# An output projection in seven block products, weight sums made by DMA, and x tiles with rows of one length

## The chip, the cores and the metric

The kernel runs on one core of one Trainium2 chip. The metric is the device time of one launch in microseconds (us). The engines are TensorE (PE in the profile; its weight loads are PEld), VectorE (DVE), ScalarE (ACT), GpSimd (POOL) and SyncE (SP), which here only issues DMAs. Each engine works through its own list of instructions in a fixed order and waits in that order.

## What is computed

One layer: 512 tokens of width 2048 and 16 meta tokens ahead of them, 8 pairs of attention heads in a sliding window, 8 groups of a state-space mixer (SSD), an output projection and a norm. Cut to what matters here:

```python
h = concatenate([meta, x])                       # 528 rows, 2048 wide
proj = rmsnorm(h, norm_pre_w) @ w_in             # z, xbc, dt, q, k, v, gate
y   = ssd(silu(conv(xbc)), dt) ; y = rmsnorm_per_group(y * silu(z)) * ssd_norm_w   # 2048 wide
att = banded_sink_attention(rope(q), rope(k), v) * silu(g_att)                      # 1024 wide
mix = concatenate([y, att])                      # 512 tokens x 3072
out = x + rmsnorm(mix @ w_out, norm_post_w)      # w_out is 3072 x 2048
```

All of it is float32. A float32 product is made of three matmuls in a rounded format (fp32r): each operand is split into a rounded part (hi) and the rest (lo), and hi·hi, hi·lo and lo·hi are summed in PSUM.

## The kernel before

**Weights.** `w_in` is read as 68 tiles, each in two chunks of 512 KB, and `w_out` as 48 chunks. A chunk n is loaded by SP's queue into `st` (two buffers), ACT rounds it to `hi` (line 132), and DVE makes `lo` = st − hi (line 133); `hi` and `lo` have three buffers each. `use(n)` asks for the split of chunk n+2 and the load of chunk n+4 and hands chunk n to the matmuls.

**Stages.** A prologue normalises and transposes x into the resident tiles `xh` and `xl` (four tiles each, four of the 16 k-blocks to a tile; a tile's row is `X_ROW[q]` floats long, of which 528 are used). Then come the keys and values, 8 attention heads (pairs of heads, in fact; "head" below is one such pair), 8 SSD groups of two units, and the output projection. A head needs two `w_in` tiles, q and gate; each is one `project(False)` of 48 matmuls 512 columns wide (16 k-blocks, three terms, line 157), written to a PSUM bank `pa`. A tile for the SSD convolutions is `project(True)`: pairs of matmuls `pa` and `pb`, 272 and 256 columns wide.

**Side work of a head** (`attend`): when its q tile is complete, four ACT copies make `swq` (467), DVE applies rope (`qr`, 469 to 471), ACT and DVE split the result into `qs` (521, 522); PE makes the scores `sc` (541, 542); DVE takes maxima `mx`, ACT exponentials into `pbuf` (550), DVE divides (`pbuf`, 557); PE transposes (`ptm` 563, `ptp` 572), ACT copies them to `pt` (575); PE multiplies with v (`av`, 590), and DVE applies the gate (`ma`, 596).

**Side work of an SSD unit**: DVE and ACT make the decay tiles `R`; PE transposes x (`xp`), DVE scales it (`xd`, and `xe` on POOL), PE makes `yd` and the states' sums `stp`, DVE runs the recurrence over four blocks (`sta`), PE makes `yo`, and DVE gathers `yy`; each group ends with a mean square by PE (`ms`), a reciprocal and two products.

**Order.** The program's order interleaves side work with projections by a clock of its own: `tick(us)` advances it by each matmul group's planned time, `spawn` starts a task, and a task's `yield us` says when it goes on. The order on each engine is then made by the tile framework's scheduler when the kernel is built: it goes by its own estimate of when each instruction's inputs are there, those of DMAs too. On the chip the order is fixed.

**Output projection.** Four column blocks of 512 (r), each over 24 k-blocks and four token blocks (t) into four PSUM banks: 4 x 24 x 4 x 3 = 1152 matmuls 128x512 (line 880). The split activations `mh` and `ml` are made once, in the first block. After each block ACT squares and DVE multiplies by the norm's weights (894, 895); the last block ends token block by token block with `finish`.

The lines that the texts below speak of most:

```python
    def use(n):
        split_w(n + (2 if n == NCI else 3))
        load(n + 3 + NST)
        return ready.pop(n)
```

Of the kernel before, what the change touches and what calls it, by code (L numbers as in the profile page):

```python
# [15 lines left out]
P = 128  # L16
D = 2048
# [10 lines left out]
NST = 2  # L28

X_ROW = (640, 576, 544, 528)  # L30
# [13 lines left out]
def hybrid_layer(ctx, tc, x, pre, npre, w_in, w_dt, par, w_out, npost, cst, out):  # L44
# [25 lines left out]
    cw = cpool.tile([P, 32, 4], F32, name="cw")  # L70
# [39 lines left out]
    NCH = NCI + 4 * (NKO // 2)  # L110
    staged, ready = {}, {}
    nload, nsplit = [0], [0]

    def load(upto):
        while nload[0] < min(upto, NCH):
            n = nload[0]
            st = wpool.tile([P, 1024], F32, tag="st", bufs=NST, name=f"st{n}")
            if n < NCI:
                src = w_in[n // 2, :, 1024 * (n % 2):1024 * (n % 2 + 1)]
            else:  # L120
                src = w_out[(n - NCI) // (NKO // 2), (n - NCI) % (NKO // 2)]
            nc.sync.dma_start(st, src)
            staged[n] = st
            nload[0] += 1
# [12 lines left out]
    def use(n):  # L137
        split_w(n + (2 if n == NCI else 3))
        load(n + 3 + NST)
# [5 lines left out]
    for q in range(4):  # L145
        for xs_, nm in ((xhg, "xh"), (xlg, "xl")):
            xs_.append(xpool.tile([P, 4, X_ROW[q]], F32R, name=f"{nm}{q}")[:, :, 0:T])
# [35 lines left out]
    with sb("pro", side="right") as pp:  # L183
# [116 lines left out]
        with tc.manual_schedule(engines={ET.PE, ET.Activation, ET.DVE, ET.Pool}):  # L300
# [59 lines left out]
            nc.vector.tensor_scalar(cw.rearrange("p a b -> p (a b)"), pr[:, P_CW:P_CW + P], 0.5, None, ALU.mult)  # L360
# [25 lines left out]
    def steps():  # L386
# [42 lines left out]
        en = sp.tile([P, P], F32, name="en")  # L429
# [5 lines left out]
        ec = sp.tile([P, P], F32, name="ec")  # L435
# [65 lines left out]

    keys(0, pieces0)
# [9 lines left out]
    def attend(hp, pieces):  # L512
# [120 lines left out]
    pools = {}  # L633
# [54 lines left out]
    def unit_task(u_, xs, cT):  # L688
# [127 lines left out]
    mh, ml = [None] * NKO, [None] * NKO  # L816
    vpool.release()
    xpool.release()
    o1 = ctx.enter_context(sb("o1", reuse_waits="tile"))
    o2 = []  # L820
    xr = [None] * NT

    def o_pool(k):
        if k < 16:
            return o1
        if not o2:
            assert not tasks
            pools["s"].release()
            o2.append(tc.alloc_tile_pool(name="o2", bufs=1, side="right", reuse_waits="tile"))
        return o2[0]  # L830

    with tc.high_priority(offset=400):
        splitting([0, 1])
    npw = ssq = None
    ot = {}
    n3 = None
    NC = NKO // 2

    def finish(t, jk):

        b = 3
        rs = o1.tile([P, 2], F32, tag="ors", bufs=4, name=f"ors{t}")
        nc.vector.tensor_reduce(rs[:, 0:1], ssq[:, t, 0:3], AX.X, ALU.add)
        nc.vector.tensor_scalar(rs[:, 0:1], rs[:, 0:1], 1.0 / D, EPS, ALU.mult, ALU.add)
        nc.scalar.activation(jk, pss[t], AF.Square, accum_out=ssq[:, t, 3:4])
        nc.scalar.activation(rs[:, 1:2], ssq[:, t, 3:4], AF.Sqrt, bias=rs[:, 0:1], scale=1.0 / D)
        nc.vector.tensor_tensor(ot[b, t], pss[t], npw[:, b * 512:(b + 1) * 512], ALU.mult)
        nc.vector.reciprocal(rs[:, 1:2], rs[:, 1:2])
        for b in range(4):
# [127 lines left out]
```

## Time and profile before

| | us |
|---|---|
| median of 3 runs (lowest, highest) | 1206.51 (1205.87, 1207.91) |
| the profiled execution | 1206.65 |
| its span in the trace | 1204.9 |
| PE busy in the span | 1192.1 |
| DVE, ACT, POOL busy | 676.4, 442.8, 48.5 |
| output projection, first to last matmul | 935.4 to 1197.3 |

The span is what the trace covers; the profiled execution's time has 1.75 us more, outside of the trace. Times inside the trace count from the span's start. The attention stage lies at about 58 to 310 us and the SSD stage at about 310 to 935 us.

### The profile page before, as it was taken

How to read it: one execution, taken by the hardware profiler on the slowest of the kernel's cores; microseconds unless marked ns; L12 is line 12 of the kernel's file. 1: busy time of each engine (PE TensorE's matmuls, PEld its weight loads, DVE VectorE, ACT ScalarE, POOL GpSimd, SP SyncE). 2: the span in 40 equal slices, each digit the busy share in tenths (PEclk: the TensorE clock that was granted, in tenths of full speed). 3: DMA queues.
4: the chain of work that ended last, by engine and by line, in shares of the span. 5: the costliest groups of instructions: out<-in, count | busy, mean ns of one | idle time of the engine just before them, and what ended most of it. 6: DMA issues, size and time to landing. Idle time of an engine off the chain costs nothing.

```text
span 1204.9 us, 18243 instructions
## 1 busy us (share of the span) xinstructions
PE 1192.1 (99%) x7565; PEld 1058.1 (88%) x7565; DVE 676.4 (56%) x1196; ACT 442.8 (37%) x754; POOL 48.5 (4%) x84
## 2 busy tenths in 40 slices
PE   8999999999999999999999999999999999999997
PEld 6998888888999989999999899998998788888886
DVE  7655555555556766656658557576675922222325
ACT  7544544445422423424234233242332712121212
POOL 0000000000100001010000000100100000000000
PEclk9999999999999999999999999999999999999999
DMA  6332222222323233233333232323332423233534
GB/s 228 100 97 88 71 86 73 71 76 91 115 95 111 91 106 99 96 108 104 105 98 97 95 116 88 114 86 105 109 97 70 157 88 104 92 101 94 169 101 179
DMA packets 37045, 125.53 MB, mean 104 GB/s; under 512 B 4706, under 2 KB 5346, under 8 KB 36706
## 3 DMA queue, kind: packets, MB, share of 16 engines
q1 hardware_dynamic: 32864, 111.78, 28.5%
q0 software_dynamic: 4096, 12.59, 3.3%
q8 instruction: 59, 0.97, 0.3%
q14 instruction: 24, 0.19, 0.1%
q10 hardware_dynamic: 2, 0.01, 0.0%
HBM read 120.03 MB, written 4.33 MB: 103 GB/s over the span
## 4 chain that ended last, share of the span: by engine, by line
PE 98%; DMA 1%; DVE 0%; ACT 0%; SPq 0%; issue 0%; DVEq 0%
PE pa L157 48%; PE po L880 22%; PE pb L157 17%; PE yd L722 1%; PE av L590 1%; PE stp L732 1%; PE yo L745 1%; PE ptp L572 1%; PE xt L228 1%; PE sc L542 1%; PE cbp L649 1%; DMA x<-in_x 1%; PE xp L702 1%; PE sc L541 1%; PE stp L730 1%; PE warm L278 0%
## 5 line engine op out<-in xcount | busy, mean ns | idle before, releaser
L133 DVE TENSOR_TENSOR lo<-st,hi 128x1024 fp32r<-128x1024 f32 x182 | 222.7, 1224 | 379.9 <-ACT hi L132 376.7
L157 PE MATMUL pa<-xh,hi 128*128 128x272 f32 (+2 forms) x1088 | 374.7, 344 | 0.0
L157 PE MATMUL pa<-xl,hi 128*128 128x272 f32 (+2 forms) x1088 | 366.1, 336 | 0.0
L157 PE MATMUL pa<-xh,lo 128*128 128x272 f32 (+2 forms) x1088 | 365.8, 336 | 0.0
L132 ACT CAST hi<-st 128x1024 fp32r<-128x1024 f32 x182 | 191.4, 1052 | 471.6 <-PE po L880 169.0
L157 PEld LDWEIGHTS pa<-xh,hi 128*128 128x128 f32 x1088 | 205.5, 189 | 24.5 <-issue 3.9
L157 PEld LDWEIGHTS pa<-xh,lo 128*128 128x128 f32 x1088 | 205.4, 189 | 21.4
L157 PEld LDWEIGHTS pa<-xl,hi 128*128 128x128 f32 x1088 | 205.3, 189 | 19.0
L157 PE MATMUL pb<-xh,lo 128*128 128x256 f32 x576 | 162.6, 282 | 0.0
L157 PE MATMUL pb<-xl,hi 128*128 128x256 f32 x576 | 162.4, 282 | 0.0
L157 PE MATMUL pb<-xh,hi 128*128 128x256 f32 x576 | 162.3, 282 | 0.0
L880 PE MATMUL po<-hi,mh 128*128 128x512 f32 x384 | 149.5, 389 | 1.2 <-ACT mh L783 1.2
L880 PE MATMUL po<-lo,mh 128*128 128x512 f32 x384 | 149.4, 389 | 0.0
L880 PE MATMUL po<-hi,ml 128*128 128x512 f32 x384 | 148.9, 389 | 0.0
L157 PEld LDWEIGHTS pb<-xh,hi 128*128 128x128 f32 x576 | 108.5, 188 | 1.1
L157 PEld LDWEIGHTS pb<-xl,hi 128*128 128x128 f32 x576 | 108.4, 188 | 0.0
L157 PEld LDWEIGHTS pb<-xh,lo 128*128 128x128 f32 x576 | 108.4, 188 | 0.0
L880 PEld LDWEIGHTS po<-hi,mh 128*128 128x128 f32 x384 | 72.1, 188 | 16.2 <-ACT mh L783 1.4
L880 PEld LDWEIGHTS po<-lo,mh 128*128 128x128 f32 x384 | 72.1, 188 | 15.0
L880 PEld LDWEIGHTS po<-hi,ml 128*128 128x128 f32 x384 | 72.1, 188 | 15.0
L626 DVE SCALAR_TENSOR_TENSOR cv<-ub,cw,cv 128x528 f32<-128x528 f32 (+1 forms) x96 | 73.4, 764 | 2.4
L627 ACT ACTIVATE ct<-cv 128x528 f32<-128x528 f32 (+1 forms) x32 | 20.5, 641 | 67.1 <-DVE cv L626 67.0
(210 smaller groups left out, 1067.6 us busy)
## 6 DMA issues: line engine op xcount, KB each, us to landing
st<-in_w_in SPq DMA_DIRECT2D x136, 512.0 KB, 3.7
st<-in_w_out SPq DMA_DIRECT2D x48, 512.0 KB, 3.5
R<-scr POOLq DMA_DIRECT2D x32, 256.0 KB, 3.6
x<-in_x SPq DMA_DIRECT2D x8, 512.0 KB, 9.4
ev<-scr POOLq DMA_DIRECT2D x32, 128.0 KB, 3.0
out<-o SPq DMA_DIRECT2D x16, 256.0 KB, 2.4
xr<-in_x SPq DMA_DIRECT2D x8, 256.0 KB, 6.6
npw<-in_npost SPq DMA_DIRECT2D x1, 1024.0 KB, 4.4
```

The source lines that it names most:

```text
L132: nc.scalar.copy(hi, st)
L133: nc.vector.tensor_tensor(lo, st, hi.bitcast(F32), ALU.subtract)
L157: nc.tensor.matmul(ps, wt, xt[k][:, a:b], start=(k == 0 and j == 0), stop=(k == NKT - 1 and j == 2))
L228: nc.tensor.transpose(tp[:, kk, :], xts[j][:, k * P:(k + 1) * P], ident)
L541: nc.tensor.matmul(sv[:, c, o0:o1], lq, kh[:, kv, t0:t0 + o1 - o0], start=True, stop=False)
L542: nc.tensor.matmul(sv[:, c, o0:o1], lq, kl[:, kv, t0:t0 + o1 - o0], start=False, stop=True)
L572: nc.tensor.transpose(tp[:, sl * P:(sl + 1) * P], src, ident)
L590: nc.tensor.matmul(av[h * 64:h * 64 + 64, j * P:(j + 1) * P], lt, rh, start=(s_ == 0), stop=(s_ == 1))
L626: nc.vector.scalar_tensor_tensor(d, uu[:, tap + c0:tap + T], cw[:, ct, tap:tap + 1], d, ALU.mult, ALU.add)
L627: nc.scalar.activation(th[:, 0:n], d, AF.Tanh)
L649: nc.tensor.matmul(cbp[:, j * P:(j + 1) * P], bT[:, cs], cT[:, cs], start=True, stop=True)
L880: nc.tensor.matmul(pss[t], a[k][:, cs], w_, start=(k == 0 and i == 0), stop=(k == NKO - 1 and i == 2))
```

## The change

**Seven products.** mix and w_out are each seen as 2 x 2 blocks (tokens by k, k by columns), and the output's four blocks come from seven block products and sums (the Strassen-Winograd form) in place of eight products. A product p has 12 chunks, 2 token blocks, 2 k-blocks to a chunk and 3 terms: 7 x 144 = 1008 matmuls 128x512, 12 for a chunk in place of 24. So 84 chunks of 512 KB are loaded and split in this stage in place of 48, with four `st` buffers there in place of two. Activation blocks and their sums are split for each product (`held`), and `done` adds the products into the output's blocks, in PSUM and SBUF, ahead of the norm.

**Weight sums.** Four of the seven products need sums of blocks of w_out. They are made in DRAM (`wsum`) during the attention stage: 24 copies of 1 MB by SP's queue and 24 accumulating DMAs of 1 MB by POOL's queue, in three tasks of six moves, 30.0 apart on the program's clock. The copies are kept in program order on SP.

**x tiles.** All eight have rows of 576 floats (2304 bytes), in place of 640, 576, 544 and 528 (2560, 2304, 2176 and 2112 bytes). Some constants share space.

```diff
-X_ROW = (640, 576, 544, 528)
+X_ROW = 576
...
-    NCH = NCI + 4 * (NKO // 2)
+    NCH = NCI + 7 * KH
...
+    W_SRC = [w_block(0, 0), wsum[1], w_block(1, 0), wsum[0], wsum[2], w_block(1, 1), wsum[3]]
...
-            st = wpool.tile([P, 1024], F32, tag="st", bufs=NST, name=f"st{n}")
+            if n % 4 > 1 and "o" in pools:
+                st = pools["o"].tile([P, 1024], F32, tag="st", bufs=2, name=f"st{n}")
+            else:
+                st = wpool.tile([P, 1024], F32, tag="st", bufs=NST, name=f"st{n}")
...
+    def weight_sums(c):
...
+        w11, w12, w21, w22 = [w_block(r, q) for r in range(2) for q in range(2)]
+        for moves in (((2, w22, None), (0, w12, None)), ((2, w12, ALU.add), (0, w11, ALU.add)),
+                      ((1, wsum[2], None),), ((1, w11, ALU.add),), ((3, wsum[1], None),), ((3, w21, ALU.add),)):
+            for d, src, op in moves:
+                for b in range(2):
+                    to, fr = wsum[d, b, c:c + 2], src[b, c:c + 2]
+                    if op is None:
+                        tc.keep_in_program_order(nc.sync.dma_start(to, fr))
+                    else:
+                        nc.gpsimd.dma_start(to, fr, accum_op=op, max_dma_last_dim=4096)
+            yield 30.0
+
+    for c in range(0, KH // 2, 2):
+        spawn(weight_sums(c), 6.0 + 25.0 * c)
...
+    def held(p, i):
...
+        if p == 1:
+            sums(i)
+        elif p == 4:
+            nc.vector.tensor_tensor(h1[:, :, HI], h1[:, :, LO], h1[:, :, HI], ALU.subtract)
+        elif p == 5:
+            nc.vector.tensor_tensor(s2[i], s2[i], h2[:, :, LO], ALU.subtract)
+        src = (h1[:, :, LO], s2[i], h2[:, :, LO], s1[i], h1[:, :, HI], s2[i], h2[:, :, HI])[p]
...
+        nc.scalar.copy(ah, src)
+        nc.vector.tensor_tensor(al, src, ah.bitcast(F32), ALU.subtract)
...
+    def done(p, t, b, ps):
...
+        elif p == 4:
+            c = oo[t + 2, b + 2] = o_tile(f"c22_{t}_{b}")
+            nc.vector.tensor_tensor(c, vv[t, b], ps, ALU.subtract)
+            nc.vector.tensor_tensor(uu[t, b], ps, uu[t, b], ALU.subtract)
+            weigh(t + 2, b + 2, c)
...
+        else:
+            if b == 1:
+                presum(t + 2)
+            c = oo[t + 2, b] = uu[t, b]
+            nc.vector.tensor_tensor(c, ps, c, ALU.add)
+            weigh(t + 2, b, c)
+            if b == 1:
+                finish(t + 2, 1)
```

**What stands where on the engines.** The scheduler's order in the attention stage and the first SSD groups is another one, since it reckons with the new DMAs. First PE, at the third head's scores (`sc_0_1656`; in the kernel before these scores are `sc_0_1637`). Before, from the end of its q tile (`pa_1456`):

```order
L157 MATMUL pa_1456<-xh_98,hi_1367 128x512
L157 MATMUL pa_1456<-xl_99,hi_1367 128x512
L157 MATMUL pa_1456<-xh_98,lo_1368 128x512
L157 MATMUL pa_1562<-xh_92,hi_1457 128x512
L157 MATMUL pa_1562<-xl_93,hi_1457 128x512
L157 MATMUL pa_1562<-xh_92,lo_1458 128x512
```

The gate's tile `pa_1562` follows here, 39 of its 48 matmuls with `av` of the head before among them, then the scores, the gate's last 9 and 33 of the next tile, and only then the transposes. After the change PE has this, in the first piece from the end of the q tile (`pa_1470`), in the second from the end of the scores:

```order
L171 MATMUL pa_1470<-xh_98,hi_1381 128x512
L171 MATMUL pa_1470<-xl_99,hi_1381 128x512
L171 MATMUL pa_1470<-xh_98,lo_1382 128x512
L573 MATMUL sc_0_1656<-kh,qs_1575 128x80
L574 MATMUL sc_0_1656<-kl,qs_1575 128x80
```

```order
L573 MATMUL sc_3_1686<-kh,qs_1575 128x192
L574 MATMUL sc_3_1686<-kl,qs_1575 128x192
L595 MATMUL ptm_1770<-ident,pbuf 16x128
L604 MATMUL ptp_0_1775<-ident,pbuf 128x128
L595 MATMUL ptm_1770<-ident,pbuf 16x128
```

The scores stand right behind the q tile that they are made from, the transposes right behind the scores, and `av` right behind the transposes, with the whole gate tile (`pa_1580`) after them. Counted for all eight heads: the projection matmuls between q and scores, scores and first transposes, last transposes and `av` were 48, 42, 21 for the first head, 36 to 39, 42, 21 for the second to the seventh, and 39, 75, 12 for the eighth. They are now 48, 42, 21 for the first; 36, 12, 0 for the second; 0, 0, 0 for the third and the fifth; 39, 9, 0 for the fourth; 39, 42, 6 for the sixth; 0 (`av` of the sixth alone is between), 0, 0 for the seventh; and 39, 75, 12 for the eighth.

Second ACT, at the copies of the second head's transposes (`pt`). Before, and then after:

```order
L132 CAST hi_1457<-st_1310 128x1024
L605 ACTIVATE gt_1453<-pa_1305 128x512
L132 CAST hi_1487<-st_1371 128x1024
L575 COPY pt_0_1509<-ptp_0_1504 128x512
L575 COPY pt_1_1516<-ptp_1_1511 128x512
L575 COPY pt_2_1532<-ptp_2_1527 128x512
L575 COPY pt_3_1537<-ptp_3_1534 128x256
```

```order
L638 ACTIVATE gt_1467<-pa_1319 128x512
L607 COPY pt_0_1527<-ptp_0_1522 128x512
L607 COPY pt_1_1534<-ptp_1_1529 128x512
L607 COPY pt_2_1550<-ptp_2_1545 128x512
L607 COPY pt_3_1555<-ptp_3_1552 128x256
L146 CAST hi_1320<-st_1228 128x1024
L146 CAST hi_1381<-st_1258 128x1024
```

The next chunks' casts have moved behind the copies; the subtractions that make `lo` stand behind them on DVE, for the second and the fourth head behind the gate product `ma` too, which reads `av`. The casts stand so at the second to the fifth and at the seventh head.

Third DVE, in the first SSD group. Before, the recurrence `sta` of the first unit is followed by a convolution and chunks' subtractions; after the change, 18 subtractions and 17 operations of convolutions stand ahead of it, 720 projection matmuls stand on PE between the first and the second row of `stp`, and behind it comes:

```order
L147 TENSOR_TENSOR lo_4682<-st_4525,hi_4681 128x1024
L769 COPY sta_3582<-stp_3577 128x128
L772 SCALAR_TENSOR_TENSOR sta_3582<-sta_3582,cdec,stp_3577 128x64 x6
L716 TENSOR_SCALAR R_0_3664<-R_0_3664,acs 128x128 x2
L742 TENSOR_TENSOR xd_3768<-xp_3759,dt 128x512
L781 TENSOR_TENSOR ev_3503<-yo_3692,ev_3503 128x512
L739 TENSOR_TENSOR xmd_3766<-xm_3764,dtm 16x128
L782 TENSOR_TENSOR yy_3557<-yy_3557,ev_3503 128x512
L758 SCALAR_TENSOR_TENSOR yy_3814<-cv_3656,pr,yd_3805 128x512
```

Four units' chains stand one behind the other there, with 123 DVE operations (4 of them subtractions for chunks) against 217 projection matmuls on PE, up to the first transpose of the fifth unit (`xp_5062`). From the third group on the order is as before.

## Rows read from the trace of the kernel before

**Rows 1.** The page, part 1: busy time of each engine.

```profile
PE 1192.1 (99%) x7565; PEld 1058.1 (88%) x7565; DVE 676.4 (56%) x1196; ACT 442.8 (37%) x754; POOL 48.5 (4%) x84
```

**Rows 2.** Waits of PE in the whole span: total, times, longest.

```profile
PE nw L295 <- DMA nwr<-in_npre: 2.7, 1, 2.7
PE xt L228 <- DVE x L219: 1.3, 1, 1.3
PE po L880 <- ACT mh L783: 1.2, 1, 1.2
```

**Rows 3.** The chain that ended last, 158 to 216: start, us, what.

```profile
159.24 0.04 PE sc L541
...
161.00 9.65 PE pa L157 x42
170.65 0.22 PE ptm L563 x2
170.87 0.87 PE ptp L572 x8
...
173.84 0.66 PE ptp L572 x6
...
179.31 2.04 PE av L590 x32
```

**Rows 4.** Timeline of DVE, 148 to 184: start, us, engine, line, operation.

```profile
164.40 1.84 DVE L557 TENSOR_SCALAR pbuf<-pbuf,sm 128x80 f32<-128x80 f32 x8
...
181.40 0.69 DVE L596 SCALAR_TENSOR_TENSOR ma<-av,gs 128x512 f32<-128x512 f32 x1 [0.19 <-PE av L590]
182.13 1.41 DVE L522 TENSOR_TENSOR qs<-qr,qs 64x512 fp32r<-64x512 f32 x2
```

**Rows 5.** Timeline of ACT, 148 to 184.

```profile
171.35 1.08 ACT L575 COPY pt<-ptp 128x512 f32<-128x512 f32 x2 [1.85 <-PE ptp L572]
...
175.74 1.05 ACT L132 CAST hi<-st 128x1024 fp32r<-128x1024 f32 x1 [0.56 <-ACT pt L575]
176.81 2.35 ACT L467 COPY swq<-pa 32x512 f32<-32x512 f32 x4
```

**Rows 6.** The chain that ended last, 930 to 1205.

```profile
947.72 249.57 PE po L880 x1101
```

**Rows 7.** Timeline of PE, 499 to 511: k-blocks 3, 9 and 15 of one projection.

```profile
501.59 0.39 PE L157 MATMUL pa<-xh,hi 128*128 128x512 f32 x1
...
505.67 0.40 PE L157 MATMUL pa<-xh,hi 128*128 128x512 f32 x1
...
509.84 0.39 PE L157 MATMUL pa<-xh,hi 128*128 128x512 f32 x1
```

**Rows 8.** Groups of DVE's instructions, 330 to 930, by shape: busy, mean ns, idle before.

```profile
L133 DVE TENSOR_TENSOR lo<-st,hi 128x1024 fp32r<-128x1024 f32 x92 | 112.6, 1224 | 144.3 <-ACT hi L132 144.0
L626 DVE SCALAR_TENSOR_TENSOR cv<-ub,cw,cv 128x528 f32<-128x528 f32 x72 | 55.3, 769 | 1.6
L773 DVE RECIPROCAL rs<-rs 128x512 f32<-128x512 f32 x7 | 23.4, 3346 | 0.0
```

**Rows 9.** The chain that ended last, 380 to 480: pairs, then one unit's small matmuls.

```profile
436.60 0.13 PE pa L157
436.84 0.13 PE pa L157
...
437.83 1.02 PE yd L722 x16
...
441.66 0.86 PE stp L732 x6
...
451.73 0.89 PE yo L745 x8
```

**Rows 10.** Windows of 1 us at the end: busy times, granted clock, DMA share, GB/s.

```profile
1197.00:1198.00 1.00, 0.28 (x2) 0.00 (x0) 0.49 (x1) 0.69 (x2) 0.00 (x0) 1.00 1.03 381
...
1200.00:1201.00 1.00, 0.00 (x0) 0.00 (x0) 1.00 (x3) 0.00 (x0) 0.00 (x0) 0.95 0.56 207
1201.00:1202.00 1.00, 0.00 (x0) 0.00 (x0) 0.57 (x1) 0.00 (x0) 0.00 (x0) 0.50 1.03 383
```

**Rows 11.** Timeline of DVE in the output projection and at its end.

```profile
1056.96 1.22 DVE L133 TENSOR_TENSOR lo<-st,hi 128x1024 fp32r<-128x1024 f32 x1 [4.21 <-ACT hi L132]
...
1198.03 0.69 DVE L847 TENSOR_TENSOR o<-po,npw 128x512 f32<-128x512 f32 x1 [0.54 <-ACT ojk L845]
1198.64 0.15 DVE L848 RECIPROCAL ors<-ors 128x1 f32<-128x1 f32 x1
1198.83 2.74 DVE L850 SCALAR_TENSOR_TENSOR o<-o,ors,xr 128x512 f32<-128x512 f32 x4
```

**Rows 12.** The page, parts 3 and 6: DMA queue SP, and its loads.

```profile
q1 hardware_dynamic: 32864, 111.78, 28.5%
...
st<-in_w_in SPq DMA_DIRECT2D x136, 512.0 KB, 3.7
```

More of the change, by code (lines that the diff above doesn't have):

```diff
@@ L834, in hybrid_layer @@
[L834 to L849, printed above, removed]
-            nc.vector.scalar_tensor_tensor(ot[b, t], ot[b, t], rs[:, 1:2], xr[t][b], ALU.mult, ALU.add)
-            nc.sync.dma_start(out[t * P:(t + 1) * P, b * 512:(b + 1) * 512], ot[b, t])
@@ L906, in hybrid_layer, with sums @@
-    o2[0].release()
+    pools["o"] = o1 = ctx.enter_context(sb("o1", reuse_waits="tile"))
+    LO, HI = slice(0, 256), slice(256, 512)
+    NP = KH // 2
+    s1, s2 = [None] * NP, [None] * NP
+    def sums(i):
+        h1, h2 = mix[i], mix[NP + i]
+        s1[i] = o1.tile([P, 2, 256], F32, name=f"s1_{i}")
+        s2[i] = o1.tile([P, 2, 256], F32, name=f"s2_{i}")
+        nc.vector.tensor_tensor(s1[i], h2[:, :, HI], h1[:, :, HI], ALU.subtract)
+        nc.vector.tensor_tensor(s2[i], s1[i], h1[:, :, LO], ALU.add)
@@ new lines, in residual, with finish @@
+    def residual(t):
+        pool, nb = (mapool, 4) if t < 2 else (pools["y"], 8)
+        for h in range(2):
+            xq = pool.tile([P, 2, S], F32, tag="m", bufs=nb, name=f"xr{t}_{h}")
+            nc.sync.dma_start(xq.rearrange("p a b -> p (a b)"), x[t * P:(t + 1) * P, h * 1024:(h + 1) * 1024])
+            xr[t, 2 * h], xr[t, 2 * h + 1] = xq[:, 0], xq[:, 1]
+    def finish(t, last):
+        nc.scalar.activation(rs[t][:, 1:2], ssq[:, t, 3:4], AF.Sqrt, bias=rs[t][:, 0:1], scale=1.0 / D)
+        nc.vector.reciprocal(rs[t][:, 1:2], rs[t][:, 1:2])
+        for b in [b for b in range(4) if b != last] + [last]:
+            nc.vector.scalar_tensor_tensor(oo[t, b], oo[t, b], rs[t][:, 1:2], xr[t, b], ALU.mult, ALU.add)
+            nc.sync.dma_start(out[t * P:(t + 1) * P, b * 512:(b + 1) * 512], oo[t, b])
@@ new lines, in hybrid_layer @@
+    tb = [(t, b) for t in range(2) for b in range(2)]
+    for p in range(7):
+        pss = {v: bank((pj, wk)[p % 2], f"po{p}_{v[0]}{v[1]}") for v in tb}
+        last = 3 if p == 6 else 1
+        order = [(i, t) for i in range(KH - last) for t in range(2)]
+        order += [(i, t) for t in range(2) for i in range(KH - last, KH)]
+        wts = {}
+        for i, t in order:
+            if i not in wts:
+                wts[i] = use(NCI + p * KH + i)
+                if i % 2 == 0:
+                    n = p * NP + i // 2
+                    for m in range(n + 1, min(n + 3, 7 * NP)):
+                        if m not in ops:
+                            ops[m] = held(m // NP, m % NP)
+                if p == 5 and i in (0, 2):
+                    residual(i // 2)
+                if p == 6 and i in (2, 4):
+                    residual(1 + i // 2)
+            hi, lo = wts[i]
+            ah, al = ops[p * NP + i // 2]
+            b = i % 2
+            cs = slice(t * P, (t + 1) * P)
+            for kk in range(2):
+                ws = slice(kk * 512, (kk + 1) * 512)
+                for j, (a, w_) in enumerate(((ah, hi), (ah, lo), (al, hi))):
+                    nc.tensor.matmul(pss[t, b], a[:, kk, cs], w_[:, ws], start=(i < 2 and kk == 0 and j == 0),
+                                     stop=(i >= KH - 2 and kk == 1 and j == 2))
+                tick(0.68)
+            if i >= KH - 2:
+                done(p, t, b, pss[t, b])
@@ L907, in hybrid_layer @@
+    pools["c"].release()
     pools["y"].release()
```

148 lines of the change are left out of this document (64 added, 84 removed).

## The prediction

> **What bounds the kernel now.** I read the page first: TensorE is busy for 1192.1 of 1204.9 us [rows 1]. The view of PE's waits has three rows, 5.2 us in all, two of them in the prologue and one at the start of the output projection [rows 2]: in the attention and SSD stages PE never waits. So a matmul that goes away is worth its time, and every wait that appears on PE is added in full. The chain that ended last shows how the attention stage keeps PE busy: behind the scores (end at 161.00) come 42 projection matmuls in 9.65 us, then transposes and more projections, then `av` [rows 3]; meanwhile DVE divides `pbuf` until 164.40 + 1.84 = 166.24 [rows 4]. PE goes on to the transposes at 170.65, 4.4 us after what they need is there. This cover is what I follow through the change.
>
> **Products.** The chain has 1101 matmuls in 249.57 us, 0.2267 us each [rows 6]. 1152 − 1008 = 144 fewer: **−32.6 us**. A chunk is now used in 12 x 0.2267 = 2.72 us, and its load (3.7 us from issue to landing [rows 12]) has four buffers, its cast takes 1.05 [rows 5], so neither ACT nor the loads bind.
>
> DVE is tighter. Before, it idles 4.21 us of each 5.44 between two `lo` of 1.22 in the projection's middle [rows 11]; now a `lo` comes each 2.72 us, and with an `al` each second chunk it is busy for some 1.5 of 2.72. The output sums come in bursts: twelve operations of some 0.61 us (a 512-wide one starts 0.61 after the one before it [rows 11]) at the end of the fifth product, 7.3 us; and in the sixth product's end two `finish` of 2.74 besides eight others, 10.4 us. The rest of DVE's time, 1.2 of each 2.72 us, and two chunks split ahead (5.4 us) must take that. I put the waits at 0 for the fifth, 3 for the sixth, 1 for the dense start: **+4** (1 to 8).
>
> **The end.** Before, after the last matmul one product (0.69), a reciprocal and 2.74 of final sums follow [rows 11]. Now the last two token blocks each have two sums, two products and 2.74; the first block's list stands ahead of the second's on DVE. Its matmuls end 18 x 0.2267 = 4.1 us before the second's, its list takes 4 x 0.61 + 0.15 + 2.74 = 5.3. So the second's starts 1.2 late, and it has three more operations (1.8): **+3** (1 to 4).
>
> **x tiles.** In one projection 512 wide, k-blocks 3 to 8 take 18 matmuls in 505.67 − 501.59 = 4.08 us (0.2267 each), 9 to 14 take 509.84 − 505.67 = 4.17 (0.2317) [rows 7]; k-blocks 4 to 7 are the tile that has 2304-byte rows already. At the fast pace for the slow seven k-blocks, 21 x 0.005 x 32 such projections = **−3.4** (0 to −4.5).
>
> **Attention.** Here the moved instructions decide. In the new order most heads have lost their cover, and PE, which waits in order, stands.
>
> - *Scores to `av` without cover* (third, fifth, seventh head). Divides end 5.24 us after the scores [rows 3, 4]; then two transposes (0.22), a `pt` copy (0.54 [rows 5]) and the last quarter of `av` (0.51) make 6.5; if the four copies queue up behind one another, 7.3. PE's own part is 0.22 + 0.87 + 0.66 + 2.04 = 3.8 [rows 3]. The wait is 2.7 to 3.5, I take 3.2. With 12 or 9 matmuls of 0.23 in between (second and fourth head) 0.45 and 1.1 remain.
> - *q to scores without cover* (third, fifth). The first copy `swq` starts at 176.81 [rows 5], `qs` ends at 182.13 + 1.41 = 183.54 [rows 4]: 6.7 us. At the seventh head `av` (2.04) stands between, and `ma` ahead of rope on DVE: 5.1.
> - *`av` to the next chunk.* `hi` (1.05) stands behind the copies and `lo` (1.22) behind it [rows 5, 8], at two heads behind `ma` (0.69 [rows 4]) too. Less two matmuls that need no `lo` and the overlap with `av`, 1.3 at three heads, 1.5 at two.
>
> Sum: 1.95 + 11.2 + 2.6 + 11.2 + 9.6 = **+36.5** (31 if the scores can begin on half of `qs`; 45 if copies queue up and each semaphore costs some tenths).
>
> **SSD.** PE runs 720 projection matmuls ahead, which costs nothing itself, but leaves four units' chains in a row. DVE's 123 operations there at the mean times of their kinds (four `lo` at 1.224, 16 convolution steps at about 0.71, seven last ones at 0.69, two reciprocals at 3.346 [rows 8], the others 0.27 to 0.75) make 69.3 us; by starts, which lie 0.08 closer [rows 11], 59.5. PE has 169 narrow projection matmuls (a pair in 0.24 [rows 9]), 48 wide ones, and small ones from 0.86 to 1.02 for a unit's `yd`, `stp` and `yo` [rows 9]: 20.7 + 10.9 + 16.7 = 48.3. DVE becomes the bound: +11 to +21. The turns of the chain between PE, DVE and ACT lie mostly inside DVE's busy time, so I take a value near the lower end, **+13**.
>
> **The clock.** After the last matmul at 1197.3 the granted clock is 1.00, until it drops to 0.95 in the window of 1200 to 1201 and 0.50 from 1201 [rows 10], 1.2 in place of 2.4 GHz, with PE idle in between. The waits of 6.7 and 5.1 us are longer than that stretch. If the clock falls in them, the scores, `av` and the first matmuls behind run at half speed: for three heads 0.9 each (scores, of which DVE's pace hides half) to 6.5 (with `av`, 2.0, and 16 projection matmuls, 3.6); I take 3, **+9** (0 to 20). The Trainium skill, page "TensorE: Matmul & The Clock Gate" (Part 1), says that the low level is the default and that activity releases it, which speaks against this change: each such wait is paid once as a wait and again in the slow work behind it. This trace agrees on the fall; it has no fall and no rise amid the work. By the page the sum has the +9, without it the sum is 1227.
>
> **The weight sums' DMAs.** SP's queue moves 111.78 MB in 28.5% of the span [rows 12], so 1 MB takes about 3.2 us alone; four copies ahead of a load delay it by some 13 us. In the old order loads landed 4 us and more ahead of their cast, two chunks (11 us) ahead of their use, and the waits above add slack: I take **0**. The bound from above is 24 copies x 3.2 = 77 us of queue time with as much again for the adds, in some 250 us that hold 70 us of loads; they fit, but if a third of them fall on late loads, +25. The page "Collectives: The Full Stack" ("Why ReduceScatter is half of AllGather") of the Trainium skill says that an add needs two source reads and so halves the rate, by which the adds would take 154 us instead of 77; no row here shows an accumulating DMA.
>
> **Sum.** −32.6 − 3.4 + 4 + 3 + 36.5 + 13 + 9 + 0 = +29.5. The profiled execution took 1206.65, 0.14 from the median: **1236**.
>
> **Rivals.**
> 1. *The steps inside a head overlap by halves* (place: third, fifth, seventh head and the four SSD units). If scores begin on the first half of `qs` and transposes, copies and `av` run block by block as early as their inputs allow, the waits are about half, 18 in attention and 6 in SSD, each short enough that I let the clock stay: −36 + 7 + 24 = −5, 1202. It turns faster when all waits on PE in both stages stay under 29 us. For it: `sc` and `ptp` come in four blocks. Against it: rope writes all of `qr` first, and one reciprocal precedes all divides.
> 2. *Loads of w_in come late behind the copies*, also since SP waits in order for adds before some copies: +25 at the chunks that have 2 to 4 copies ahead, 1260. Against it: the slack above.
> 3. *The clock stays up* because scores and transposes still trickle: 1227.
>
> **How the numbers follow.** Forecast (1222 to 1250) 0.60; rival 1 0.11; rival 2 0.15; rival 3 0.14. The bounds of the terms, taken together, give 1212 and 1270. The range 1212 to 1262 leaves out rival 1 and the upper part of rival 2. A measurement of this kernel tells 0.2% (2.4 us) from no change. Rival 1 alone holds the faster side, 0.08, and no change, 0.03; slower 0.89.
>
> **What would show it.** Output matmuls at 0.2267, 1008 of them. In PE's waits: two of about 6.7 us at `sc` behind ACT or DVE `qs`, one of 5, waits at `ptp` and `av` on `pbuf` and `pt`, and at projections on `lo`. A granted clock under 1.00 in windows at the third, fifth and seventh head. DVE close to full for some 60 us where PE is not, in the first SSD groups. No wait on `st`. Wrong would be: waits of PE under 29 us in sum, or large ones on DMA.

## The result and the profile after

The changed kernel takes **1255.04 us** (median of 4 runs, 1254.06 to 1257.94); the kernel before took 1206.84 beside it. The ratio is 1.0403, 95% interval 1.0383 to 1.0424. The prediction was 1236, range 1212 to 1262. The profiled execution is the slowest of the four, 1257.94 us, with a span of 1255.4.

The page, part 1, of the kernel after, beside [rows 1]:

```profile
PE 1182.9 (94%) x7421; PEld 1047.8 (83%) x7421; DVE 761.9 (61%) x1302; ACT 491.4 (39%) x812; POOL 70.9 (6%) x108
```

144 matmuls are gone, but PE's busy time fell by 9.2 us only, and 72.5 us of the span are idle, where it was 12.8. Waits of PE, in total, times, longest (beside [rows 2], which had three rows):

```profile
PE sc L573 <- DVE qs L554: 21.6, 4, 7.0
PE ptm L595 <- DVE pbuf L589: 11.6, 5, 2.9
PE pa L171 <- DVE lo L147: 6.3, 8, 1.3
PE yd L754 <- DVE xd L742: 3.9, 2, 3.4
...
PE pa L171 <- ACT hi L146: 2.6, 2, 2.1
```

The three largest are the three kinds that the prediction lists for attention. PE's timeline in the third head, beside [rows 3]:

```profile
161.64 0.39 PE L171 MATMUL pa<-xh,lo 128*128 128x512 f32 x1
169.02 0.41 PE L573 MATMUL sc<-kh,qs 128*128 128x80 f32 x1 [6.99 <-DVE qs L554]
...
175.66 0.37 PE L595 MATMUL ptm<-ident,pbuf 128*16 128x128 f32 x1 [2.94 <-DVE pbuf L589]
...
176.25 2.98 PE L604 MATMUL ptp<-ident,pbuf 128*128 128x128 f32 x13
...
179.78 2.35 PE L622 MATMUL av<-pt,vt 128*64 128x128 f32 x28
182.06 0.50 PE L171 MATMUL pa<-xh,hi 128*128 128x512 f32 x1
```

q ends at 162.03, nothing covers the chain to `qs`, and PE stands for 6.99 us, then 2.94 us for the divides. DVE shows what it waited for, beside [rows 4]: rope at once when ACT's copies are done, then `qs`, with nothing of the transfers in between:

```profile
164.44 0.69 DVE L483 TENSOR_TENSOR qr<-pa,rt 128x512 f32<-128x512 f32 x1 [12.06 <-ACT swq L481]
...
167.47 1.40 DVE L554 TENSOR_TENSOR qs<-qr,qs 64x512 fp32r<-64x512 f32 x2 [1.02 <-ACT qs L553]
...
175.25 1.84 DVE L589 TENSOR_SCALAR pbuf<-pbuf,sm 128x80 f32<-128x80 f32 x8
```

The clock, in windows of 2 us around the same stall (busy us and count of PE, PEld, DVE, ACT, POOL; granted clock; DMA share; GB/s), beside [rows 10]:

```profile
160.00:162.00 2.00, 2.00 (x9) 1.33 (x8) 0.00 (x0) 0.00 (x0) 0.00 (x0) 1.00 1.04 276
162.00:164.00 2.00, 0.03 (x1) 0.00 (x0) 0.00 (x0) 1.90 (x4) 0.00 (x0) 1.00 1.09 229
164.00:166.00 2.00, 0.00 (x0) 0.00 (x0) 1.53 (x3) 0.41 (x1) 0.00 (x0) 0.50 1.07 213
...
180.00:182.00 2.00, 2.00 (x28) 1.89 (x26) 1.27 (x2) 1.64 (x2) 0.00 (x0) 0.74 0.00 0
182.00:184.00 2.00, 2.00 (x12) 1.61 (x9) 1.09 (x1) 0.00 (x0) 0.00 (x0) 1.00 0.47 102
```

PE stops at 162.03, the clock is at half from the window that begins at 164, and it rises again inside the one from 180 to 182 (0.74): the scores and transposes run at 1.2 GHz, and `av` for the most part. The clock is at half in six stretches of the stages up to the first SSD groups: behind a wait at the first, third, fifth and seventh head, and twice in the SSD stage.

```profile
112.78:116.19 3.41, 3.41 (x16) 3.31 (x16) 3.41 (x8) 2.03 (x6) 0.00 (x0) 0.50 0.40 114
163.98:181.04 17.06, 9.08 (x48) 8.16 (x50) 9.36 (x29) 8.56 (x26) 0.00 (x0) 0.50 0.47 93
239.07:252.72 13.65, 7.19 (x32) 6.61 (x32) 8.26 (x27) 6.25 (x22) 1.23 (x2) 0.50 1.04 213
307.34:320.99 13.65, 8.50 (x42) 7.57 (x44) 7.07 (x25) 7.55 (x24) 0.00 (x0) 0.50 0.61 121
382.43:385.84 3.41, 3.41 (x18) 3.41 (x17) 0.22 (x1) 0.54 (x1) 0.00 (x0) 0.50 0.88 280
553.10:563.33 10.23, 8.62 (x39) 7.44 (x35) 8.89 (x20) 1.79 (x4) 2.10 (x4) 0.50 0.16 53
```

PE is busy in them for 40.2 us. A head's 16 scores take 3.70 us at half clock (third head) and 1.94 at full (fourth head), so about half of the 40.2, some 20 us, is what the low clock adds; this is an estimate from these rows. By stage (scores of the first head to the SSD stage, the SSD stage's first groups with one stretch of them apart, and the rest of it):

```profile
112.00:401.00 289.00, 252.28 (x1475) 215.92 (x1476) 130.28 (x297) 112.98 (x264) 22.06 (x28) 0.91 0.80 215
401.00:600.00 199.00, 185.82 (x1284) 169.19 (x1283) 113.52 (x190) 57.34 (x82) 14.84 (x23) 0.97 0.28 88
540.00:600.00 60.00, 51.31 (x346) 45.12 (x346) 56.48 (x106) 25.68 (x38) 8.81 (x13) 0.91 0.26 85
600.00:1013.00 413.00, 412.28 (x2979) 383.28 (x2977) 269.99 (x468) 138.43 (x195) 30.02 (x49) 1.00 0.32 102
```

PE is idle for 289.00 − 252.28 = 36.7 us in the first stretch and for 199.00 − 185.82 = 13.2 in the second; in the 60 us from 540 DVE is 94% busy and PE 86%. Last, the transfers in 58 to 310 (KB each, median us to landing), beside [rows 12]:

```profile
wsum<-in_w_out POOLq DMA_DIRECT2D x22, 1024.0 KB, 24.6
st<-in_w_in SPq DMA_DIRECT2D x29, 512.0 KB, 8.4
wsum<-in_w_out SPq DMA_DIRECT2D x12, 12.9
wsum<-wsum SPq DMA_DIRECT2D x10, 15.8
```

Loads take 8.4 us there in place of 3.7. ACT waits for them in 58 to 401 (without the sums it has no such wait in these stages), while PE's own waits on `hi` in the whole span make 2.6 us:

```profile
ACT hi L146 <- DMA st<-in_w_in: 47.2, 13, 9.5
```

At the first head such a wait reaches PE all the same. The copies `swq` of its q stand on ACT behind a cast whose load is late, and its scores wait 2.88 us for `qs`, although all 48 matmuls of their cover are in place:

```profile
104.65 1.05 ACT L146 CAST hi<-st 128x1024 fp32r<-128x1024 f32 x1 [3.33 <-DMA st<-in_w_in]
105.73 2.35 ACT L481 COPY swq<-pa 32x512 f32<-32x512 f32 x4
```

### The profile page after: what moved, and what is told of

Read it like the earlier page. It is cut to its first block, busy times and chain, and to the rows that moved or that the text cites. A ratio compares the mean times of both kernels' runs of the same rounds, so it can differ in the third digit from the quotient of the medians.

```text
span 1255.4 us, 18358 instructions
## 1 busy us (share of the span) xinstructions
PE 1182.9 (94%) x7421; PEld 1047.8 (83%) x7421; DVE 761.9 (61%) x1302; ACT 491.4 (39%) x812; POOL 70.9 (6%) x108
## 5 line engine op out<-in xcount | busy, mean ns | idle before, releaser
L147 DVE TENSOR_TENSOR lo<-st,hi 128x1024 fp32r<-128x1024 f32 x218 | 265.5, 1222 | 285.8 <-ACT hi L146 285.1
L146 ACT CAST hi<-st 128x1024 fp32r<-128x1024 f32 x218 | 228.2, 1050 | 404.7 <-PE pb L171 167.8
L171 PEld LDWEIGHTS pa<-xl,hi 128*128 128x128 f32 x1088 | 206.0, 189 | 18.7
L980 PE MATMUL po<-lo,ah 128*128 128x512 f32 x336 | 131.1, 390 | 1.3 <-DVE lo L147 1.3
L980 PE MATMUL po<-hi,ah 128*128 128x512 f32 x336 | 129.7, 389 | 1.2 <-ACT ah L872 1.2
L980 PE MATMUL po<-hi,al 128*128 128x512 f32 x336 | 130.2, 389 | 0.0
L980 PEld LDWEIGHTS po<-lo,ah 128*128 128x128 f32 x336 | 63.1, 188 | 15.5 <-DVE lo L147 2.5
L659 DVE SCALAR_TENSOR_TENSOR cv<-ub,pr,cv 128x528 f32<-128x528 f32 (+1 forms) x96 | 74.1, 772 | 2.2
L980 PEld LDWEIGHTS po<-hi,ah 128*128 128x128 f32 x336 | 63.1, 188 | 14.4 <-ACT ah L872 1.4
L980 PEld LDWEIGHTS po<-hi,al 128*128 128x128 f32 x336 | 63.1, 188 | 13.0
```

The lines of the kernel that those rows point to most:

```text
L146: nc.scalar.copy(hi, st)
L147: nc.vector.tensor_tensor(lo, st, hi.bitcast(F32), ALU.subtract)
L171: nc.tensor.matmul(ps, wt, xt[k][:, a:b], start=(k == 0 and j == 0), stop=(k == NKT - 1 and j == 2))
L659: nc.vector.scalar_tensor_tensor(d, uu[:, tap + c0:tap + T], cw[:, ct, tap:tap + 1], d, ALU.mult, ALU.add)
L980: nc.tensor.matmul(pss[t, b], a[:, kk, cs], w_[:, ws], start=(i < 2 and kk == 0 and j == 0), stop=(i >= KH - 2 and kk == 1 and j == 2))
```

## Experiments

The theory behind the prediction (order): the sums' DMAs move covers out of attention and bunch the SSD chains when the kernel is built, and the waits, with the clock that falls in them, are the loss. The rival (transfers): the traffic itself delays what PE needs.

**1. No sums.** Products and x rows stay; the four products that need sums read plain blocks of w_out, so that part of the result is left out.

```diff
-    W_SRC = [w_block(0, 0), wsum[1], w_block(1, 0), wsum[0], wsum[2], w_block(1, 1), wsum[3]]
+    W_SRC = [w_block(0, 0), w_block(0, 1), w_block(1, 0), w_block(0, 0), w_block(1, 1), w_block(1, 1), w_block(0, 1)]
...
-        spawn(weight_sums(c), 6.0 + 25.0 * c)
```

> The changed kernel without the 24 copies and 24 accumulating DMAs; the four products that need summed weights read plain blocks of w_out in their place, so that part of the result is left out. PE's order in the attention and SSD stages is that of the kernel before. Theory 1 (all of the loss comes with the sums of weights, through the order and the clock): PE does not wait in those two stages, the granted clock stays 1.00 there, and the time is 1206.8 - 32.6 - 3.4 + 3 to 7 for DVE and the end = 1174 to 1178 us. Rival (the output projection or the x tiles cost the time themselves): 1200 us or more.

**1176.02 us** (5 runs), ratio 0.9744 (0.9731 to 0.9757). PE by the page, and in attention and the SSD stage:

```profile
PE 1156.6 (98%) x7421; PEld 1030.5 (88%) x7421; DVE 761.3 (65%) x1302; ACT 492.2 (42%) x812; POOL 48.5 (4%) x84
```

```profile
107.00:341.00 234.00, 234.00 (x1473) 201.16 (x1473) 128.59 (x295) 112.00 (x263) 4.36 (x8) 1.00 0.28 85
341.00:933.00 592.00, 591.11 (x4261) 549.39 (x4260) 383.54 (x657) 197.27 (x277) 43.97 (x72) 1.00 0.33 101
```

So the rest of the change gains 30.5 us and the sums lose 79.0. This kernel also splits the loss. The idle time differs by 72.5 − 18.7 = **53.8**. The 7421 matmuls are the same, but PE is busy with them for 1182.9 us in the changed kernel and for 1156.6 here, **26.3** less. About 20 of these are the half clock estimated above. The other 6 lie where PE stops, which it does 36 times more often: the last matmul ahead of a stop counts with its whole 0.39 us, and not with the 0.2267 after which the next one would start (36 x 0.16 = 5.8).

**2. No sums, old x rows.**

```diff
-X_ROW = 576
+X_ROW = (640, 576, 544, 528)
```

> As the run without sums (the same part of the result is left out), with the x tiles' rows as before (640, 576, 544, 528 floats). Theory (the slow k-blocks are those whose row isn't 2304 or 2560 bytes): 3.4 us slower than the run without sums, with 18 matmuls of k-blocks 9 to 14 in 4.17 us where that run has 4.08. Rival (the slow pace has another cause, such as the bank or the place in the chunk): the same time within 0.5 us.

1179.79 us (4 runs), ratio 0.9776 (0.9763 to 0.979): the rows are worth 3.8 us; 3.4 was forecast. The two kernels' runs do not overlap (1178.58 to 1180.9 here, 1175.02 to 1177.27 with rows of one length).

**3. Copies on POOL's queue**, free to be placed by the scheduler.

```diff
-                        tc.keep_in_program_order(nc.sync.dma_start(to, fr))
+                        nc.gpsimd.dma_start(to, fr)
```

> The changed kernel with the 24 copies of the weight sums issued on POOL's queue in place of SP's. All 48 DMAs and their bytes remain. PE's order in the attention stage is that of the kernel before; in the first SSD groups the chains of four units are still compressed behind some 670 projection matmuls. Theory 1 (order): the attention stage's waits of 36 us and its half clock go, the SSD's 13 us and a few us of half clock stay: 1176 + 13 + 4 = about 1193 us. Theory 2 (the transfers themselves make w_in's loads late): the loads are still late, PE waits on hi and lo, and the time stays above 1215 us.

1285.64 us (4 runs), ratio 1.0652: by the number the rival's side, but not at the rival's place. Nothing held the copies back, so they began with the program, and the DMA engines were full for the first 250 us. The x loads landed after 33.7 us (9.6 in the changed kernel), and the first scores came at 182.4 (112.4 in the changed kernel, 106.8 without sums). PE's largest wait, and its stretch from first scores to the SSD stage:

```profile
PE xt L242 <- DVE x L233: 32.6, 3, 15.7
```

```profile
182.00:424.00 242.00, 235.74 (x1479) 201.88 (x1478) 126.40 (x280) 110.22 (x260) 8.59 (x12) 1.00 0.47 136
```

Attention has its covers again and loses 6.3 us idle, its clock at 1.00. That speaks for the order in attention; but full DMA engines cost much where loads have no slack. The SSD chains are bunched as in the changed kernel: from the first `cbp` to the output projection this kernel takes 613.6 us, the changed one 612.4, the one without sums 592.1.

**4. Fillers**: matmuls whose product nobody reads, 20, 20 and 18 ahead of the scores and 12 behind them, at the three heads without cover.

```diff
+        if hp in (2, 4, 6):
+            wp = bank(wk, f"fill{hp}")
+            for _ in range(20 if hp < 6 else 18):
+                nc.tensor.matmul(wp, last_hi[0][:, 0:P], xh[0][:, NM:T], start=True, stop=True)
...
+        if hp in (2, 4, 6):
+            wp = bank(wk, f"fil2{hp}")
+            for _ in range(12):
+                nc.tensor.matmul(wp, ones, xh[0][:, NM:T], start=True, stop=True)
```

> The changed kernel with matmuls 128x512 of no use put into PE's waits at the third, fifth and seventh head: 20, 20 and 18 between the q tile and the scores, 12 between the scores and the transposes. The results are the same. Theory 1 (the excess over the waits is the clock at half speed): granted clock 1.00 from 160 to 330 us, PE's waits there smaller by what the fillers fill, the stage's other matmuls at full speed: 1255 - 15 to 22 = 1233 to 1240 us. Rival (the clock's fall costs nothing since PE waits for DVE and ACT then anyway): 1253 to 1258 us.

1252.49 us (4 runs), ratio 1.0378 (1.0364 to 1.0393): close to the rival's number. The whole of attention, and two windows elsewhere:

```profile
111.00:396.00 285.00, 268.50 (x1569) 225.43 (x1570) 129.43 (x296) 111.74 (x263) 22.13 (x28) 0.97 0.82 218
```

```profile
112.00:116.00 4.00, 4.00 (x16) 3.71 (x16) 3.96 (x13) 2.16 (x10) 0.00 (x0) 0.50 0.97 279
...
284.00:288.00 4.00, 4.00 (x14) 3.24 (x14) 2.62 (x11) 3.43 (x17) 0.88 (x1) 0.57 1.04 374
```

The clock stayed at 1.00 at the three heads, but fell behind shorter waits at other heads. With 94 fillers of 0.2267 taken off (21.3), PE is busy for 247.2, which is 13.2 over the 234.0 of the kernel without sums; the changed kernel is 18.3 over. At the three heads, the stretch from the end of the q tile to the first projection behind `av` takes 16.8, 16.6 and 16.7 us in place of 20.0, 19.0 and 19.8. But the edit did more than fill: the scheduler moved `av` of the second and the fourth head behind the fillers of the next one's q tile, with a wait of 1.75 us in its old place each time, and the sixth head's scores wait 2.43 us where they had no wait. So the 2.6 us gained are what is left of both; they do not bound what the low clock costs at the three heads.

**5. SSD freed, and its control without sums.** The work that queued behind the adds on POOL goes to other engines; attention is left as it is.

```diff
-            nc.gpsimd.dma_start(R, scr[0, 2 * u_ + h].partition_broadcast(P))
+            nc.sync.dma_start(R, scr[0, 2 * u_ + h].partition_broadcast(P))
...
-        nc.gpsimd.tensor_tensor(xe, xd[:, 0:NT - 1],
+        nc.vector.tensor_tensor(xe, xd[:, 0:NT - 1],
...
-            nc.gpsimd.dma_start(ev[64 * h:64 * h + 64], scr[1, h0 + h].partition_broadcast(64))
+            nc.sync.dma_start(ev[64 * h:64 * h + 64], scr[1, h0 + h].partition_broadcast(64))
```

> The changed kernel with one part undone: R and ev are issued by SyncE and xe is computed by VectorE for all units, so that the first groups of the SSD stage no longer queue behind the adds on POOL; attention keeps the changed kernel's order. Nothing is left out. Order theory: the SSD stage's loss of some 13 us of idle time and 4 us of low clock is given back and attention's is not: 1237 to 1243 us; against the kernel before about 1.025 to 1.030. Transfer theory: the sums' traffic still runs into the SSD stage's first groups, so no more than 5 us come back: 1250 to 1256 us.

> A control for the two others: the kernel without the sums (the output projection reads plain w_out blocks in their place, so its result isn't the reference's), with R and ev on SyncE's queue and xe on VectorE. What the move costs by itself: 16 xe of some 0.5 us more on VectorE, of which none is on TensorE's path by the trace of before: 1174 to 1179 us, as without the move (1176.0). If VectorE's or SyncE's queue is too full for it, up to 1190 us.

1231.89 us (4 runs), ratio 1.0211 (1.0196 to 1.0226); the control 1175.77 (4 runs), so the move itself costs nothing. Attention and the SSD stage's first groups:

```profile
113.00:396.00 283.00, 248.56 (x1475) 212.44 (x1476) 130.22 (x297) 112.99 (x264) 17.57 (x20) 0.92 0.82 219
396.00:591.00 195.00, 195.00 (x1378) 180.47 (x1377) 128.29 (x223) 64.21 (x91) 0.00 (x0) 1.00 0.33 100
```

23 us come back, 5 more than the most that was expected: the SSD stage's first groups have no idle time and a full clock again, while attention still idles for 283.00 − 248.56 = 34.4 us. PE's matmuls stand again as without the sums in these groups; whether the chains were slow for the wait on POOL itself or for the order that the scheduler built around it, this run does not tell.

**6. Same order, sums late.** All copies and adds on POOL, in six parts that wait for the gated tiles of the second to seventh head; R, ev and xe as in 5. PE's order is that of the kernel without sums.

```diff
+        if 0 < hp < 7:
+            weight_sums(hp - 1, m)
...
+        nc.gpsimd.dma_start(wsum[2, b, c][:, 0:512], src_tile)
+        for d, src in ((2, w22), (0, w12), (1, w11), (3, w21)):
+            tc.keep_in_program_order(nc.gpsimd.dma_start(wsum[d, b, c:c + 2], src[b, c:c + 2]))
+        for d, src in ((2, w12), (0, w11), (1, wsum[2]), (3, wsum[1])):
+            nc.gpsimd.dma_start(wsum[d, b, c:c + 2], src[b, c:c + 2], accum_op=ALU.add, max_dma_last_dim=4096)
```

> Nothing is left out: the same 24 copies and 24 adds, but all are issued by POOL, four copies and then four adds in each of six parts, each part held back by a small transfer out of the gated tile of an attention head (second to seventh head); R and ev go to SyncE's queue and xe to VectorE for all units, so that the sums hold nothing up on POOL. The matmuls of TensorE stand in the order of the kernel without the sums. Order theory (the loss came from covers moved out of the waits between a head's matmuls): the time comes back to that of the kernel without the sums plus a few us, 1177 to 1188 us, and scores come 2 us at most behind the stall-free place. Transfer theory (the sums' traffic of some 75 MB delays weight loads and the scratch transfers, whoever issues it): still above 1195 us, with idle time of TensorE before projections.

**1245.36 us** (4 runs), ratio 1.034 (1.0287 to 1.0393). Here the order theory fails as a full account: with PE's order whole in both stages, the traffic cost 69 us. From 350 to 450 the DMA engines are full and PE is busy for two thirds of the time; ACT's wait for weight loads in 106 to 460, DVE's wait in 350 to 450, and a landing time there:

```profile
350.00:400.00 50.00, 30.98 (x193) 27.92 (x193) 20.65 (x40) 10.31 (x16) 6.81 (x10) 0.82 1.01 265
```

```profile
ACT hi L146 <- DMA st<-in_w_in: 66.4, 10, 10.4
```

```profile
DVE R L710 <- DMA R<-scr: 36.1, 5, 14.6
```

```profile
R<-scr SPq DMA_DIRECT2D x4, 256.0 KB, 12.2
```

Two paths carry the loss. Weight loads come late to ACT's casts, and DVE's `lo` comes behind them; what stands next in the order of these two engines reaches PE late: the transposes of two heads (4.1 and 4.3 us), the scores of one (5.2) and `yd` of two units (6.9 and 10.3). And the decay rows `R` are on the SSD chain and land 12.2 us after issue, where they took 3.8 without sums; PE waits 4.3 and 7.6 us at projections, whose cast and `lo` stand behind `R`, and 6.3 at `yo`. The profiled execution is the slowest of the four, 1257.8; some 12 us of it are waits in the output projection, about what it has above the median.

**7. Sums through SBUF.** Blocks of w_out are loaded into tiles that are empty at that time, added by POOL and stored, 24 MB each way. Eight half chunks in attention, the other sixteen, as eight whole ones, in the SSD stage.

```diff
+    def weight_sums(tiles, c, b, cols):
+        for t, (row, col) in zip(tiles, ((1, 1), (0, 1), (0, 0), (1, 0))):
+            nc.gpsimd.dma_start(t, w_block(row, col)[b, c][:, cols])
+        for d, s in ((0, 1), (1, 2), (2, 0), (3, 2)):
+            nc.gpsimd.tensor_tensor(tiles[d], tiles[d], tiles[s], ALU.add)
+        for d, t in zip((2, 0, 1, 3), tiles):
+            nc.gpsimd.dma_start(wsum[d, b, c][:, cols], t)
```

> Nothing is left out: the weight sums are made by another way. Each quarter of w_out is loaded into SBUF (tiles of the mix that are still empty: two pairs of heads in the attention stage, the last four groups in the SSD stage), added there on POOL and stored, all from POOL's queue, so that 24 MB are read and 24 MB written in place of copies and adds from DRAM to DRAM; it begins when the first keys are there and is paced by the tiles themselves. R and ev go to SyncE's queue and xe to VectorE. The matmuls of TensorE stand in the order of the kernel without the sums. If order alone made the loss: 1176 to 1182 us. If order and the share of the DMA engines made it together (sums_on_pool_late kept the order and stood at 1245, with the DMA engines full for 250 us): with the share at some 0.6 to 0.7 in place of 1.0 the weight loads keep their slack, and 1178 to 1195 us. If any such traffic beside the stages costs its time: above 1205 us.

1221.56 us (4 runs), ratio 1.0124 (1.0108 to 1.0141): better, but above the first two expectations and in the third, that any such traffic costs its time. The last runs below decide against that one. The SSD stage's start, and the groups of DVE's `R` in 350 to 450, first here, then without sums (mean ns is the number ahead of the second bar):

```profile
351.00:480.00 129.00, 104.89 (x669) 96.22 (x668) 108.56 (x109) 31.96 (x46) 89.22 (x74) 0.88 0.77 281
```

```profile
L720 DVE TENSOR_SCALAR R<-R,acs 128x128 f32<-128x128 f32 x16 | 14.0, 933 | 4.8 <-DMA R<-scr 4.8
```

```profile
L714 DVE TENSOR_SCALAR R<-R,acs 128x128 f32<-128x128 f32 x24 | 5.4, 280 | 4.7 <-DMA R<-scr 4.7
```

The same operation takes 933 ns instead of 280 on average: a cost that neither theory had. By single instructions of this trace, the 117 `R` operations that no add of POOL overlaps take 0.27 to 0.35 us, at full DMA engines too, and the 11 that one overlaps 0.53 to 2.84.

**8. All sums in attention**, alternating between two sets of tiles.

> Nothing is left out: the sums as in sums_through_sbuf, but all 24 half blocks in the attention stage, after the first values are there, through two sets of tiles that are empty then (the mix tiles of the fifth to eighth head, and four tiles of the convolution); none in the SSD stage. The matmuls of TensorE stand in the order of the kernel without the sums. In sums_through_sbuf the halves in attention took 13 us each and its stretch from the first scores to the SSD stage 238.9 us for 234.5 without sums, with the DMA engines at 0.7; the 16 later quarters of w_out cost the SSD stage some 35 us. If that loss hangs on the stage (transfers on the path and VectorE's work beside POOL's adds) it goes: 1180 to 1190 us. If it hangs on the amount of traffic, it moves with the sums: 1205 us or more, with late weight loads in attention.

1241.39 us (6 runs), ratio 1.0301. The forecast was wrong, mostly by one tile: attention takes 296.7 us, 62 more than without sums. DVE's product of the fifth head is written to a tile that POOL still used; DVE runs in order, so `qs` of the next head stood behind it. A tile of the convolution, held by POOL for 18.2 us, brought PE's other long wait. DVE's wait, and PE's two:

```profile
DVE ma L631 <- DMA wsum<-ma: 37.9, 1, 37.9
```

```profile
PE sc L574 <- DVE qs L555: 36.5, 3, 34.7
PE pa L171 <- ACT hi L146: 9.8, 1, 9.8
```

**9. Sums spread**: 17 half chunks one after the other in attention, one at the start of the SSD stage and one behind each of its first six groups.

> Nothing is left out: the sums through SBUF as in the two runs before, but spread: 17 half blocks one after the other in the attention stage (11 through the mix tiles of the fifth to eighth head, from the last keys on, then six through four tiles of the convolution), one at the start of the SSD stage, and one behind each of its first six groups. TensorE's matmuls stand in the order of the kernel without the sums. If the loss of sums_in_attention was one tile held too long (the fifth head's product waited 35 us on VectorE for POOL's sums in its tile) and that of sums_through_sbuf the density of POOL's adds in the SSD stage: 1179 to 1195 us, faster than the kernel before. If the sums cost their time wherever they stand: 1205 us or more.

1201.01 us (5 runs), ratio 0.9948 (0.9935 to 0.9962), the first below the kernel before, though above what was expected: the second set of tiles had nothing to wait for and began with the program, where POOL is busy and PE loses time. The first scores come at 125.1 us, for 106.8 without sums:

```profile
0.00:50.00 50.00, 40.81 (x246) 34.19 (x247) 36.58 (x63) 26.86 (x51) 32.07 (x39) 0.97 0.77 270
```

**10. Sums spread, later.** Ten half chunks behind the first values, five behind those, nine in the SSD stage.

```diff
+    behind(sets[0], vt[:, 0, 0:128])
+    for n in range(10):
+        weight_sums(sets[0], *halves.pop())
+    behind(sets[1], sets[0][3][:, 0:128])
+    for n in range(5):
+        weight_sums(sets[1], *halves.pop())
...
+        if g < 6:
+            behind(sets[2], mix[4 + g][:, 1, 0:128])
+            for _ in range((1, 1, 2, 2, 1, 1)[g]):
+                weight_sums(sets[2], *halves.pop())
```

`behind` is a POOL operation that reads its second argument and writes into each tile, so that the loads wait for it.

> Nothing is left out: as sums_spread, with its two early places mended: there the second set of tiles had nothing to hold it back and began with the program (first scores at 125.1 us for 106.8). Now ten half blocks run one after the other from the first values on, five more behind them, one at the start of the SSD stage and one or two behind each of its first six groups. If the sums cost only where they meet the prologue's chains and full DMA engines: the 18 us come back, 1178 to 1188 us (the kernel without sums: 1176). If they cost their time wherever they stand, what is saved ahead of the first scores is lost again in attention and the SSD stage: 1196 to 1205 us.

**1179.95 us** (5 runs), ratio **0.9788** (0.9774 to 0.9801): faster than both kernels, 3.9 us over the kernel without sums. PE in attention, the DMA engines at 0.64:

```profile
106.00:341.00 235.00, 235.00 (x1478) 201.91 (x1478) 154.40 (x299) 112.89 (x264) 140.44 (x173) 1.00 0.64 213
```

## Why the prediction was right, and where its sizes were off

The direction, the places and most prices were right; the time came out 19 us above the forecast, inside its range. Two terms failed: the clock's, which was less than half of what was measured, and that of the sums' DMAs, put at nothing.

- **Products, output stage, end, x rows** (−32.6, +4, +3, −3.4: −29.0): the kernel without sums shows −30.5, the rows −3.8 of it. In the changed kernel PE is idle for 2.6 us of the 230 from 1010 (for the +4), and DVE's last sums take 6.35 us, 1245.79 to 1252.14, for the 3.54 of [rows 11] (for the +3).
- **Attention waits, +36.5**: idle 36.7 in 112 to 401. The waits at the scores of the three heads are as forecast (18.7 for 18.5), and those at transposes and `av` close to it (12.5 for 11.15). That the sum agrees so well is luck: projections behind `lo` wait 2.6 us, at the second and the fourth head, where 6.9 at five heads were forecast, and in their place the window holds 2.6 us at 380 to 382, with the SSD stage's first projections, and the end of the first head's wait. Rival 1, overlap by halves, is out: `sc` starts at 169.02, when all of `qs` is done (167.47 + 1.40).
- **SSD, +13**: idle 13.2, of which 8.7 fall in the 60 us from 540, with DVE as the bound as forecast; freeing POOL gave 23 us back, with the clock's part.
- **The clock, +9 (0 to 20)**: some 20 us, at the upper bound. At the third, fifth and seventh head it is 12.4 (half of 9.08, 7.19 and 8.50), where 3 each were taken. The other 7.7 came where the forecast let the clock stay: 1.7 at the first head, whose wait was not foreseen, and 1.7 and 4.3 in the SSD stage. Behind the waits of 1.06 to 1.70 us at the second and the fourth head it stayed at 1.00. The page "TensorE: Matmul & The Clock Gate" (Part 1) of the Trainium skill, which the prediction weighed, calls the low level the default, which activity releases. This trace agrees: the clock fell in the three long waits or soon behind shorter ones and rose again while PE worked (at 181.04 in the third head), so waits were paid again, here some 20 us on top of 53.8. Rival 3 (clock stays up) is out.
- **Stops, not in the forecast**: 6 us, the ends of the matmuls ahead of them (run 1).
- **The sums' DMAs, 0 (to +25)**: too low. The loads had slack, as was said, but it did not cover all of them. The first scores come at 112.4, 5.6 us later than without sums, of which PE's waits name 5.1: 2.9 at those scores, behind ACT's late cast, and 2.2 at `lo`, `hi` and a transpose before them. As a rule the 0 was wrong: runs 3 and 6 show the same traffic at 69 us and more where it meets chains without slack. Rival 2 had the mechanism, at a larger price than this kernel shows (25); in run 6 it costs PE some 31 us by weight loads and 18 by `R`, in run 3 it is there for the x loads.

The bounds of the terms, added up as the prediction has them, give 1213.5 and 1272 with the sums' DMAs at 0, not 1212 and 1270; the range hardly moves by it.

Sum as measured: −30.5 + 53.8 + 26.3 = 49.6, against 51.3 between the two profiled executions. The 53.8 are 3.9 ahead of 112, 36.7 in attention and 13.2 in the SSD stage.

## What to carry to other kernels

Work that is added beside a full engine costs by where the schedule puts it, not by its own time: the same sums cost 79 us, 69 us or 4 us. Check three things before adding it: whether the order of the bound engine stays the same, whether loads ahead of an in-order engine, or transfers on a dependent chain, meet full DMA engines, and whether an in-order engine waits for a tile that the new work still holds. Price a wait on TensorE at more than its length where the clock falls in it: here 53.8 us of waits brought some 20 us of half clock and 6 us of stops.

## What the hardware showed unexpectedly

- POOL's adds slow VectorE: from 280 to 933 ns on average for a 128x128 `R` (run 7), and the four `kl` operations that take 2.85 us without sums took 6.34 beside the first adds, by DVE's timeline in the same run:

```profile
69.78 6.34 DVE L499 SCALAR_TENSOR_TENSOR kl<-kr,kh 64x528 fp32r<-64x528 f32 x4
```

The Trainium skill, page "GPSIMD Engine Reference" (Specifications), says that GpSimd's SBUF interfaces are shared with VectorE, with contention for some of VectorE's instructions; these rows agree.

- An accumulating DMA of 1 MB from DRAM to DRAM lands after 24.6 us beside the loads and copies of attention, a plain copy after 12.9 to 15.8, and a 256 KB `R` after 12.2 in place of 3.8 when the DMA engines are full.
